# One layer of a diffusion backbone on one core: other weights in the list that orders the attention's instructions, and accumulators of two later stages on named banks in another turn

## The chip, the cores and the metric

One Trainium2 chip, one of its cores. The metric is the device time of one execution in microseconds (us); the median of several runs is compared. The engines are TensorE (PE: matmuls and transposes; PEld: its weight loads), VectorE (DVE), ScalarE (ACT), GpSimd (POOL) and SyncE (SP, which here only issues DMAs).

## What is computed

One layer over 1024 tokens of width 1024 with 256 context tokens, all in 32 bits:

```
h = x * (1 + scale1) + shift1                      # modulation from c
proj = h @ w_in + b_in                             # q, k, v of two branches, and gate logits
A: 8 heads, 2 kv heads, window of +-128 keys + 256 context keys, a sink logit per head
B: 8 heads, 2 kv heads, all 1024 keys + 256 context keys, RMS norm on q and k
y = (sig(ga) * (o_a @ w_branch_a) + sig(gb) * (o_b @ w_branch_b)) @ w_out
x = LN(alpha * x + gate1 * y)
h = x * (1 + scale2) + shift2
u = conv3(h @ w_up);  y = (silu(u_gate) * u_val) @ w_down
out = LN(alpha * x + gate2 * y)
```

## The kernel before, in words

A 32-bit product is made of three matmuls: each operand is split into a high part (a cast, `hi`) and a low part (operand minus high part, `lo`), and high*high, high*low and low*high are added in PSUM (`mm3`, L374 to L376). The splits are made by `split` (cast on L366, difference on L371) or, in attention, by lines of their own. PSUM has 8 banks; a tile of 128x512 fills one, a tile of 128x1024 two.

The stages run one after the other: projections and gates (0 to about 320 us of the span), attention (320 to 742), the rest of branch B's product and the output product with the first LayerNorm (742 to about 860), the up product with the convolution in 22 tiles (to about 1305), the down product and the last LayerNorm. PE runs through all of them with little idle time.

**Attention** is cut into 32 units: branch A's 16 (8 query blocks times 2 kv heads, four heads each), then branch B's 16. A unit's steps: POOL splits q (`qhi`, `qlo`, L723 and L726), PE turns it (`qtr`, L731), ACT copies it (L736), a DMA swaps its halves (`qdm`, L740); PE makes the scores of the four heads (`sc`, and in branch B `scx` for the context keys; L752 and L753); DVE scales them and takes the row minimum (`pm`, L786), ACT takes the exponential (`ex`, L795). Then, key block by key block (4 or 5 in branch A, 10 in branch B; "chunk" below), PE turns the probabilities (`tr`, L840, four transposes into one bank of the ring `pt`), the turned chunk is split, and PE multiplies it with the values (`av`, L849, one matmul for the high part and one for the low part, into the one bank `av0`). A chunk is split in one of two ways: ACT casts it out of PSUM (`hi`, L1218) and DVE subtracts (`lo`, L1224); or, for the chunks in the list `POOLED`, ACT copies it out of PSUM (`cp`, L1208) and POOL does both (`ph`, L1213, and `pl`, L1224). The first `av` of a unit starts the sum, so every other `av` of the unit is ordered behind the high part of chunk 0. At the end ACT copies the sum (`avs`, L1238), and POOL does a chain of five steps (`up` L1242, `ot` L854 twice, `tt` L1249, `oh` L866, `ol` L863). Between the units run 16 groups of branch A's output product, and at the end four of branch B's (`grp`, 12 matmuls each, tile `ptb`), whose gate is multiplied in by DVE (L1115).

The order of all this is made while the program is built. `graph` lists the operations, each with an engine, a cost and a key: the unit's number plus a weight from the list `KEY`. `plan` goes through them: for each engine it looks at the first `LOOK` operations in the order of their keys, takes those that could start within `SLACK` of the earliest, and of these the one with the least key. So a key is a priority among operations that could start at about the same time, not a date. `FILL` are the keys of the first and the last of branch A's groups. The resulting order on all five engines is fixed in the program; on the chip each engine goes through its list and waits where an operand is late.

**PSUM behind attention.** The pool `ps3` has two tags: `sml` (L1322; 2 slots of one bank) and `big` (L1319; 3 slots of two banks). In the program before, `sml` has the banks 0 and 1, and the three slots of `big` are the banks 2-3, 6-7 and 4-5, used in this turn. `big` is called 20 times: four accumulators of branch B's product, ten of the output product, and six of the first three tiles of the up product (gate and value of tiles 0, 1 and 2: `u0_0`, `u1_0`, `u0_1`, `u1_1`, `u0_2`, `u1_2`). The last three, `u1_1`, `u0_2` and `u1_2`, are on 4-5, 2-3 and 6-7. A `u` accumulator is read by one ACT instruction (L1688) and two DVE instructions (L1689, L1691) of `conv3`; then its banks are free.

From tile 3 on (`up_tile`, L1825 to L1857) a tile is seven products of four `mm3` each (A11, S2, S1, S3, A12, S4, A22: Strassen's scheme) in four accumulators a, b, c, d of one bank each. Their banks come from the list `PSU = 6, 7, 2, 3, 4, 5, 0, 1` (L50): tile 3 has a on 6, b on 7, c on 2, d on 3, and tile 4 has 4, 5, 0, 1. In this stage PE's order is that of the program; the other engines' order is arranged by the framework when the program is built.

Of the kernel before, what the change touches and what calls it, by code (L numbers as in the profile page):

```python
# [7 lines left out]
F32 = mybir.dt.float32  # L8
# [5 lines left out]
P = 128  # L14
D = 1024
T = 1024
# [23 lines left out]
PWB = 5  # L40
DAH = 3
SINK = 640
POOLED, FILL, SUMS = ((3,), (2, 6)), (16.13, 25.4), ('ot1', 'ot1')
LOOK, SLACK = 24, (0, 0, 0, 0.11, 0.209)
D3AT = (7, 5), (7, 9), (4, 1), (4, 4), (4, 7), (4, 10), (5, 2)
NXS = 5
RAWB = 3
# [38 lines left out]
def plan(ops, rings, free, look, slack):  # L86
    todo = [sorted((o for o in ops if o.eng == e), key=lambda o: o.key) for e in range(5)]
    for o in ops:
        for b in o.uses:
            b.left += 1  # L90
    port, done = 0.0, []
    while any(todo):
        best = None
        for e in range(5):
            ready = []
            for o in todo[e][:look]:
                if any(d.end is None for d in o.after):
                    continue
                r = max([free[e]] + [d.end for d in o.after] + [b.free(rings) for b in o.takes])
                if o.port:  # L100
                    r = max(r, port)
                if r < BIG:
                    ready.append((r, o))
            if ready:
                least = min(r for r, _ in ready) + slack[e]
                pick = min((c for c in ready if c[0] <= least), key=lambda c: c[1].key)
                if best is None or pick[0] < best[0]:
                    best = pick
        r, o = best
        todo[o.eng].remove(o)  # L110
        o.start, o.end = r, r + o.lat
        free[o.eng] = r + o.occ
        if o.port:
            port = r + o.occ
        for b in o.takes:
            b.slot = rings[b.ring].index(b.free(rings)) if b.fix is None else b.fix
            rings[b.ring][b.slot] = BIG
        for b in o.uses:
            b.left -= 1
            b.end = max(b.end, o.end)  # L120
            if b.left == 0:
                rings[b.ring][b.slot] = b.end
        done.append(o)
    return sorted(done, key=lambda o: o.start)
# [9 lines left out]
    tr=(PE, .436, .685), hi=(ACT, .47, .675), lo=(DVE, .605, .765), cp=(ACT, .47, .675), ph=(POOL, .59, .70),  # L134
# [9 lines left out]
PRING = "pt", "s", "av"  # L144
RINGS = dict(pt=3, s=2, av=1, qs=1, q1=2, q2=2, p=8, hi=4, lo=4, ptr=2, up=1, ot=1, rb=2, wraw=1, wh=1, wl=1)

KEY = {'qh': -2.206, 'qt': -0.961, 'sc': 0.037, 'scs': (0.029, 0.269),
           'scx': -0.548, 'tr': 0.763, 'tru': (0.17, 0.098),
           'av': 1.292, 'st': 1.191, 'out': 1.297, 'exd': 0.565, 'st1': 1.248, 'wb': (28.06, 28.638),
           'wg': (31.993, 33.356, 33.022, 33.265), 'ge': 1.33, 'gr': 4.033}  # L150
UNITS = 32


def graph(x, key=KEY, pooled=((3,), (2, 6)), fill=None, ot=("ot0", "ot1")):
    ops, last = [], {}
# [191 lines left out]
def rings():  # L347
    return {n: [0.0] * c for n, c in RINGS.items()}
# [3 lines left out]
def layer_kernel(  # L352
# [66 lines left out]
    def ht(name, shape=(P, T), dt=F32):  # L419
        hslot[name] = pool, tag = hfree.pop(0)  # L420
        return pool.tile(list(shape), dt, tag=tag, name=name, bufs=1)
# [38 lines left out]
    sc, scc = ht("sc"), ht("scc")  # L460
# [21 lines left out]
    st1 = {}  # L482
# [808 lines left out]
    rwb = {}  # L1291
    for o in plan(graph(Issue(), KEY, POOLED, FILL, SUMS)[0], rings(), [0.0, 2.2, 0.0, 0.0, 0.0], LOOK, SLACK):
        if o.fn:
# [18 lines left out]
    ps3 = tc.alloc_tile_pool(name="ps3", bufs=1, space=PSUM, reuse_waits="tile")  # L1312

    hfree += [(za, f"Z{n}") for n in range(16)]

    def tm(name, dt=F32, w=T):
        return post.tile([P, w], dt, tag="m", name=name, bufs=4)

    def big(name):  # L1319
        return ps3.tile([P, T], F32, tag="big", name=name, bufs=3)  # L1320

    def sml(name, w=512):  # L1322
        return ps3.tile([P, w], F32, tag="sml", name=name, bufs=2)
# [49 lines left out]
    wb = {2: [wq.tile([P, 8, P], R32, tag="w", name=f"{a}wb2", bufs=4) for a in "hl"]}  # L1373
# [3 lines left out]
    def both(f):  # L1377
        bT[1, f] = ht(f"bT1_{f}")
        nc.sync.dma_start(bT[1, f], sgd[KT + f])
        ps = big(f"b1_{f}")  # L1380
        w = wb[f // 2]
        for hf in (0, 1):
            for j in range(4):
                k = (f % 2) * 4 + j
                a = O[1, hf, 0, j // 2][:, j % 2], O[1, hf, 1, j // 2][:, j % 2]
                mm3(ps[:, hsl(hf)], (w[0][:, k], w[1][:, k]), a, j == 0, j == 3)
        nc.vector.tensor_tensor(out=bT[1, f], in0=ps, in1=bT[1, f], op=ALU.mult)
# [27 lines left out]
    def diag(cols, n, nm):  # L1415
        dg = tm(f"dg{nm}", w=HALF).rearrange("p (a b) -> p a b", b=P)
        i = nc.vector.tensor_tensor(out=dg[:, 0:n], in0=ident.unsqueeze(1).to_broadcast([P, n, P]),
                                    in1=cols.unsqueeze(2).to_broadcast([P, n, P]), op=ALU.mult)
        last_diag[:] = [i.ins]
        return dg[:, 0:n].rearrange("p a b -> p (a b)")  # L1420
# [7 lines left out]
    def ln_add(zf, zs, zq, s, first, nm, qe, se):  # L1428
        w = s.stop - s.start
        ln_flush()  # L1430
        if first:
            nc.scalar.activation(zq[:, s], zf, AF.Square)
            nc.gpsimd.tensor_scalar(out=zs[:, s], in0=zf, scalar1=1.0, scalar2=0.0, op0=ALU.mult, op1=ALU.add)
            return
        q = tm(f"sq{nm}", w=w)
        nc.scalar.activation(q, zf, AF.Square)
        se.tensor_tensor(out=zs[:, s], in0=zs[:, s], in1=zf, op=ALU.add)
        sqs.append(lambda: qe.tensor_tensor(out=zq[:, s], in0=zq[:, s], in1=q, op=ALU.add))
# [18 lines left out]
    def ln_steps(zs, zq, s, nm, emit, first, gap, gap1, gap2, each, pm=2, order=range(KT), behind=None):  # L1457
# [41 lines left out]
        def held(f):  # L1499
# [5 lines left out]
            for n, f in enumerate(order)]  # L1505

    zs, zq = tm("zs1"), tm("zq1")
    def wout_z(f, s, ps, first):
        nc.vector.scalar_tensor_tensor(out=zv(f, s), in0=ps, scalar=modc[:, 16 + f:17 + f], in1=zv(f, s),
# [99 lines left out]
    def y_pair(f, s, first=False):  # L1609
        w = s.stop - s.start  # L1610
        ps = big(f"y{f}_{s.start}_{w}")
        for ks in (range(6), range(6, KT)) if first and s.start == 0 else (range(KT),):
            for a in (0, 1):
                mm_ticked(ps[:, a * HALF:a * HALF + w], wts[f + a], mrg, s, ks)
        for a in (0, 1):
            wout_z(f + a, s, ps[:, a * HALF:a * HALF + w], first and a == 0)
# [94 lines left out]
    def up_start(j, gv):  # L1711
        if (j, gv) not in ups:
            if (j, gv) not in upw:
                up_weights(j, gv)
            ups[j, gv] = big(f"u{gv}_{j}"), upw.pop((j, gv)), set()
        return ups[j, gv]
# [45 lines left out]
    for k in range(4):  # L1762
        steps = build(k)
        n = 2 if k < 2 else 0
# [10 lines left out]
    ps3 = tc.alloc_tile_pool(name="ps3u", bufs=1, space=PSUM, reuse_waits="tile")  # L1775
# [415 lines left out]
```

## Time and profile before

| | us |
|---|---|
| median of 3 runs | 1541.86 (1540.32 to 1542.12) |
| profiled execution | 1540.56 |
| its span, from the first to the last instruction | 1538.8 |
| PE busy in the span | 1516.7 |
| DVE, ACT, POOL busy | 1142.5, 803.6, 780.6 |
| PE's longest wait, at about 941 us | 6.3 |

Views of the profile: *waits* lists who waited for whom; *windows* gives busy time of each engine in stretches of the span, with PE's granted clock (1.00 is full speed); *timeline* lists instructions in order of time (start, duration, engine, line, what it writes and reads, and in brackets the idle time before it and what ended it); *lines* groups instructions by line. An end of a matmul is modelled: the start of the next is the surer number.

### The profile page before, as it was taken

Reading aid. Unit: us, or ns where it says so; the run is one execution under the profiler, and the core shown is the slowest. Engines: PE = TensorE matmul, PEld = TensorE weight load, DVE = VectorE, ACT = ScalarE, POOL = GpSimd, SP = SyncE. Lnnn points to the kernel's source line nnn. Section 1 sums busy time; section 2 is a strip of 40 time slices with the busy share of each in tenths; the row PEclk is TensorE's granted clock in tenths of the full one; section 3 lists DMA queues with packets and bytes.
Section 4 is the critical chain, followed back from the end, with each engine's and each line's share of the span. In section 5 each row is a group of like instructions: output and inputs, shape, how many; then the busy total and the mean of one; then the engine's idle time right before and its main releaser. Section 6 shows DMA issues by size and latency. Waiting matters only on the chain.

```text
span 1538.8 us, 21952 instructions
## 1 busy us (share of the span) xinstructions
PE 1516.7 (99%) x7652; PEld 1271.8 (83%) x7652; DVE 1142.5 (74%) x1729; ACT 803.6 (52%) x1403; POOL 780.6 (51%) x741
## 2 busy tenths in 40 slices
PE   9999999999999999999999998999999999999997
PEld 7888888888988888888788986888888888888886
DVE  7588847628777777887656887788888787656797
ACT  5422223449977767898223563444444444435543
POOL 0375303428887565785334555666676675021063
PEclk9999999999999999999999999999999999999999
DMA  9667663312347573652471322233334446996733
GB/s 377 239 227 253 223 236 106 100 38 62 92 134 183 131 154 82 165 115 66 144 173 35 104 87 92 88 108 114 113 109 114 110 111 171 373 280 211 251 95 110
DMA packets 112161, 229.73 MB, mean 149 GB/s; under 512 B 13521, under 2 KB 27345, under 8 KB 111954
## 3 DMA queue, kind: packets, MB, share of 16 engines
q1 hardware_dynamic: 97040, 199.72, 39.7%
q0 software_dynamic: 10400, 20.19, 8.4%
q10 hardware_dynamic: 4610, 8.42, 1.5%
q8 instruction: 60, 0.98, 0.3%
q14 instruction: 51, 0.42, 0.1%
HBM read 177.09 MB, written 65.87 MB: 158 GB/s over the span
## 4 chain that ended last, share of the span: by engine, by line
PE 90%; DVE 4%; POOL 2%; issue 2%; ACT 1%; DMA 1%; DVEq 0%; SPq 0%; POOLq 0%; ACTq 0%
PE av L849 7%; PE pt L840 6%; PE g L376 4%; PE g L374 4%; PE g L375 4%; PE p L374 4%; PE p L376 4%; PE p L375 4%; PE s L752 3%; PE s L753 3%; PE a L374 2%; PE a L375 2%; PE a L376 2%; PE d L375 2%; PE c L375 2%; PE d L376 2%
## 5 line engine op out<-in xcount | busy, mean ns | idle before, releaser
L1224 DVE TENSOR_TENSOR lo<-pt,hi 128x512 fp32r<-128x512 f32 x188 | 126.1, 687 | 31.0 <-ACT hi L1218 28.5
L371 DVE TENSOR_TENSOR ld<-rd,hd 128x1024 fp32r<-128x1024 f32 x77 | 97.8, 1288 | 49.2 <-ACT hd L366 45.5
L1218 ACT CAST hi<-pt 128x512 fp32r<-128x512 f32 x188 | 108.4, 583 | 43.3 <-PE pt L840 38.1
L366 ACT CAST hd<-rd 128x1024 fp32r<-128x1024 f32 x77 | 79.6, 1052 | 84.7 <-PE p L376 60.4
L374 PE MATMUL p<-hd 128*128 128x512 f32 x264 | 103.3, 391 | 0.0
L375 PE MATMUL p<-ld,hd 128*128 128x512 f32 x264 | 102.8, 389 | 0.0
L376 PE MATMUL p<-hd,ld 128*128 128x512 f32 x264 | 102.7, 389 | 0.0
L849 PE MATMUL av<-lo,VT 128*128 128x512 f32 x236 | 100.8, 432 | 0.4 <-POOL lo L1224 0.4
L849 PE MATMUL av<-hi,VT 128*128 128x512 f32 x236 | 101.0, 435 | 0.2 <-ACT ptra L1238 0.2
L786 DVE TENSOR_SCALAR_CACHE_REDUCE p<-s,cvt,nmc 128x1024 f32<-128x1024 f32 x64 | 85.9, 1341 | 20.5 <-PE s L753 12.7
L376 PE MATMUL g<-hh,wlg 128*128 128x512 f32 x256 | 99.8, 390 | 0.4 <-POOL wlg L371 0.4
L374 PE MATMUL g<-hh,whg 128*128 128x512 f32 x256 | 100.0, 391 | 0.0
L375 PE MATMUL g<-hl,whg 128*128 128x512 f32 x256 | 99.6, 389 | 0.0
L371 POOL TENSOR_TENSOR wlg<-wg,whg 128x512 fp32r<-128x512 f32 x32 | 45.2, 1417 | 103.8 <-ACT whg L366 86.7
L795 ACT ACTIVATE p<-p,nm 128x1024 f32<-128x1024 f32 x64 | 74.1, 1158 | 17.7 <-DVE p L786 17.5
L840 PE MATMUL pt<-ident,p 128*128 128x128 f32 x512 | 76.6, 272 | 0.0
L840 PEld LDWEIGHTS pt<-ident,p 128*128 128x128 f32 x512 | 63.1, 140 | 15.7
L752 PE MATMUL s<-KL,q 128*128 128x512 f32 (+2 forms) x186 | 73.5, 395 | 0.0
L753 PE MATMUL s<-KL,q 128*128 128x512 f32 (+2 forms) x186 | 69.6, 374 | 0.5 <-DMA q<-q 0.5
L366 ACT CAST wS<-s 128x512 fp32r<-128x512 f32 x76 | 45.7, 623 | 44.7 <-POOL s L1523 41.9
L366 ACT CAST wA<-ru 128x512 fp32r<-128x512 f32 x57 | 35.6, 625 | 61.5 <-PE d L376 32.7
L786 DVE TENSOR_SCALAR_CACHE_REDUCE pa<-s,negsink 128x640 f32<-128x640 f32 (+1 forms) x58 | 49.2, 856 | 24.0 <-PE s L753 19.3
(436 smaller groups left out, 5030.7 us busy)
## 6 DMA issues: line engine op xcount, KB each, us to landing
wml<-in_wmodT_dram SPq DMA_DIRECT2D x48, 512.0 KB
ru<-in_w_up_dram SPq DMA_DIRECT2D x38, 512.0 KB
rd<-td SPq DMA_DIRECT2D x55, 256.0 KB
rd<-sd SPq DMA_DIRECT2D x44, 256.0 KB
rd<-in_w_dn_dram SPq DMA_DIRECT2D x33, 256.0 KB
wm<-in_wmodT_dram SPq DMA_DIRECT2D x16, 512.0 KB
wg<-in_w_g_dram SPq DMA_DIRECT2D x32, 256.0 KB
q<-q SPq DMA_DIRECT2D x64, 128.0 KB
```

Of the source, the lines that this page charges most:

```text
L366: cast[:] = [nc.scalar.copy(hi, src).ins]
L371: low[:] = [lo_eng.tensor_tensor(out=lo, in0=src, in1=hi.bitcast(F32), op=ALU.subtract).ins]
L374: nc.tensor.matmul(ps, a[0], b[0], start=start, stop=False, skip_group_check=resumed)
L375: nc.tensor.matmul(ps, a[0], b[1], start=False, stop=False, skip_group_check=resumed)
L376: return nc.tensor.matmul(ps, a[1], b[0], start=False, stop=stop, skip_group_check=resumed).ins
L752: nc.tensor.matmul(o, self.q1[:, hs], ks, start=True, stop=False)
L753: nc.tensor.matmul(o, self.q2[:, hs], ks, start=False, stop=stop)
L786: nc.vector.tensor_scalar(out=p if self.br else p[:, self.pad + 1:SINK + 1], in0=self.sv[h], scalar1=self.scale()[:, hs] if self.br else - ...
L840: nc.tensor.transpose(tr[:, h * P:(h + 1) * P], src, ident)
L849: nc.tensor.matmul(self.av, v, self.parts[n][low], start=first, stop=self.left == 0)
L1218: nc.scalar.copy(hi, units[u].parts[n])
L1224: e.tensor_tensor(out=lo, in0=src, in1=hi.bitcast(F32), op=ALU.subtract)
```

## The change

Two things. The weights of the planned order are replaced: `KEY`, `FILL`, `SLACK` and `POOLED`. And `big` gets three tags with one slot each in place of one tag with three; three empty tiles at the head of the pool `ps3` lay out their banks first, and a list says the turn: `big2`, `big0`, `big1`, and so on.

```diff
-POOLED, FILL, SUMS = ((3,), (2, 6)), (16.13, 25.4), ('ot1', 'ot1')
-LOOK, SLACK = 24, (0, 0, 0, 0.11, 0.209)
+POOLED, FILL, SUMS = ((0,), (1, 8)), (16.885703, 28.298765), ('ot1', 'ot1')
+LOOK, SLACK = 24, (0, 0, 0.031835, 0.0879, 0.031696)
...
-KEY = {'qh': -2.206, 'qt': -0.961, 'sc': 0.037, 'scs': (0.029, 0.269),
-           'scx': -0.548, 'tr': 0.763, 'tru': (0.17, 0.098),
-           'av': 1.292, 'st': 1.191, 'out': 1.297, 'exd': 0.565, 'st1': 1.248, 'wb': (28.06, 28.638),
-           'wg': (31.993, 33.356, 33.022, 33.265), 'ge': 1.33, 'gr': 4.033}
+KEY = {'qh': -1.21914, 'qt': -1.187093, 'sc': -0.106225, 'scs': (0.233244, 0.27861),
+           'scx': -1.945172, 'tr': 0.840531, 'tru': (0.122743, 0.070723),
+           'av': 1.36184, 'st': 1.192968, 'out': 0.661224, 'exd': 1.373419, 'st1': 1.769253, 'wb': (27.79832, 29.926055),
+           'wg': (31.897283, 33.009176, 33.189585, 33.435465), 'ge': 0.762978, 'gr': 4.580045}
...
+    bigs = [2, 0, 1]
+    for n in range(3):
+        ps3.tile([P, T], F32, tag=f"big{n}", name=f"bg{n}", bufs=1)
...
     def big(name):
-        return ps3.tile([P, T], F32, tag="big", name=name, bufs=3)
+        bigs.append(bigs.pop(0))
+        return ps3.tile([P, T], F32, tag=f"big{bigs[-1]}", name=name, bufs=1)
```

`POOLED` has one list for each branch (chunks of a unit, counted from 0). The pairs in `scs` and `tru` are branch A's and branch B's. `wb` and `wg` are the keys of the weight loads and of the groups of branch B's product at the end of attention.

## The prediction

> **What bounds the kernel now.** First the head of the page: PE is busy in 1516.7 us of 1538.8, so at most 22 us of idle time can go away, and work that PE has to do at its pace stays.
>
> ```profile
> span 1538.8 us, 21952 instructions
> PE 1516.7 (99%) x7652; PEld 1271.8 (83%) x7652; DVE 1142.5 (74%) x1729; ACT 803.6 (52%) x1403; POOL 780.6 (51%) x741
> ```
>
> Next the waits of PE, longest first (engine, line, whom it waited for, us, times, longest), which say where that idle time ends:
>
> ```profile
> PE a L374 <- DVE c L1691: 6.3, 1, 6.3
> PE b L374 <- POOL O L866: 1.2, 1, 1.2
> ...
> PE b L374 <- DVE bT L1115: 0.9, 1, 0.9
> PE s L753 <- DMA q<-q: 0.5, 1, 0.5
> PE av L849 <- POOL lo L1224: 0.4, 2, 0.3
> ```
>
> One wait stands out: the first up tile in Strassen's form (tile `a`) waits 6.3 us, once, for a convolution on DVE. Waits of attention (L753, L849) are below a microsecond each. Then busy time by stretch of attention and of what follows it (from:to, length, PE, PEld, DVE, ACT, POOL busy, granted clock, DMA share, GB/s):
>
> ```profile
> 320.00:360.00 40.00, 39.31 (x249) 34.83 (x249) 23.28 (x53) 27.08 (x61) 17.92 (x30) 1.00 0.15 37
> 360.00:400.00 40.00, 39.97 (x277) 36.19 (x276) 32.94 (x70) 35.92 (x81) 33.88 (x50) 1.00 0.32 81
> 400.00:440.00 40.00, 39.52 (x272) 35.40 (x271) 28.97 (x63) 35.10 (x79) 33.38 (x48) 1.00 0.38 105
> 440.00:480.00 40.00, 39.13 (x234) 32.16 (x233) 29.47 (x66) 30.83 (x71) 36.85 (x49) 1.00 0.65 167
> 480.00:640.00 160.00, 160.00 (x935) 134.50 (x934) 116.75 (x241) 115.09 (x247) 93.68 (x114) 1.00 0.53 129
> 640.00:720.00 80.00, 80.00 (x498) 67.03 (x497) 68.45 (x143) 72.13 (x163) 58.60 (x72) 1.00 0.52 120
> 720.00:742.00 22.00, 21.80 (x117) 17.96 (x116) 10.03 (x17) 11.19 (x23) 9.19 (x13) 1.00 0.11 34
> 742.00:755.00 13.00, 10.58 (x45) 7.86 (x44) 6.90 (x7) 2.21 (x3) 3.71 (x5) 1.00 0.62 230
> ```
>
> PE's idle time in attention is 0.69 + 0.03 + 0.48 + 0.87 = 2.1 us in branch A (to 480), 0.2 us in branch B (to 742), and 2.4 us where attention ends (742 to 755). No second engine is at its limit, but ACT and POOL come near it: 35.9 and 33.9 of 40 at 360 to 400, and at 440 to 480 POOL has 36.9 of 40.
>
> **The change, part by part. 1: the banks.** I follow the 20 calls of `big`. Before, the turn of the slots is 2-3, 6-7, 4-5; the twentieth accumulator, `u1_2`, has 6-7, and tile 3's `a` opens on bank 6. So PE can't begin tile 3 before DVE has read the very last convolution input. After, the empty tiles take 0-1, 2-3 and 4-5, so `sml` gets 6 and 7; call n (from 0) takes slot (n + 2) mod 3. `u1_1` (n = 17) gets 2-3, `u0_2` 4-5, `u1_2` 0-1. Tile 3's a and b (6, 7) then follow small LayerNorm tiles that are long done, c and d (2, 3) follow `u1_1`; `u1_2` is met first by tile 4's c, nine products (24.5 us, below) after PE's last `u` matmul instead of right behind it. Within `ps3` each call still takes the slot of the call three before it, so nothing else there waits for longer. The timeline of PE at this place:
>
> ```profile
> 940.64 0.39 PE L376 MATMUL u<-B,lwu 128*128 128x512 f32 x1
> 947.33 0.76 PE L374 MATMUL a<-B,wA 128*128 128x512 f32 x1 [6.30 <-DVE c L1691]
> ...
> 950.88 0.53 PE L376 MATMUL a<-B,wA 128*128 128x512 f32 x1
> 951.24 0.39 PE L374 MATMUL a<-B,wA 128*128 128x512 f32 x1
> 951.47 0.40 PE L375 MATMUL a<-B,wA 128*128 128x512 f32 x1
> ```
>
> The pitch from start to start is 0.23 us outside the wait (951.24 to 951.47; I reckon with 0.227, the mean over longer stretches). So PE was free at 940.64 + 0.227 = 940.87 and began at 947.33: **6.46 us**. And the nine matmuls from 947.33 to 951.24 took 3.91 us, where nine pitches are 2.04: **1.87 us** more. The granted clock says why:
>
> ```profile
> 941.00:947.30 6.30, 0.03 (x1) 0.00 (x1) 6.27 (x6) 2.35 (x4) 2.65 (x2) 0.76 0.32 87
> 947.30:951.30 4.00, 3.97 (x10) 3.18 (x11) 2.80 (x2) 0.00 (x0) 3.17 (x3) 0.52 0.69 263
> ```
>
> It is 0.76 on average in the wait and about half for 4 us behind it. The Trainium skill, "TensorE: Matmul & The Clock Gate", Part 1, says the gate halves the clock after an idle window of about 3.4 us and gives it back after about 3.4 us of work; by that the loss behind the wait would be an estimated 1.7 us, and the sum below 0.2 us smaller. The trace agrees within that; the measured 1.87 us stays.
>
> What is late next, if the bank no longer holds `a`? DVE's list there:
>
> ```profile
> 930.19 0.69 DVE L371 TENSOR_TENSOR wA<-ru,wA 128x512 fp32r<-128x512 f32 x1
> ...
> 939.56 2.97 DVE L371 TENSOR_TENSOR wS<-s,wS 128x512 fp32r<-128x512 f32 x3
> 942.45 1.75 DVE L371 TENSOR_TENSOR wA<-ru,wA 128x512 fp32r<-128x512 f32 x1
> ...
> 945.31 0.68 DVE L371 TENSOR_TENSOR wA<-ru,wA 128x512 fp32r<-128x512 f32 x1
> 945.91 1.27 DVE L1691 SCALAR_TENSOR_TENSOR c<-u,cvt,c 128x1023 f32<-128x1023 f32 x1
> ...
> 948.48 1.66 DVE L1702 TENSOR_TENSOR c<-c 128x512 f32<-128x512 f32 x1
> ```
>
> A11's weight is split by 930.9. A product is 12 matmuls, 2.72 us, so S2 would begin at 943.6, S1 at 946.3, S3 at 949.0, A12 at 951.8, A22 at 957.2. The three S splits end at 942.5 and the A splits at 946.0, all in time. `d` is full at 951.8 and must be read by DVE before A22: DVE's list ends at 950.1, with two additions of 0.69 us (as the first row, of the same shape) left, so by about 953, 4 us before it is needed. That list is the cover; were 4 us of DVE work put ahead of the read, A22 would begin to wait. Behind 951.5 no wait of PE over 0.2 us is in the list until the end, and loads of later weights start when PE frees their slots, so they move with it. I take the whole **-8.3 us**; 0 if the layout is not as I derive it.
>
> **2: the end of attention.** PE's timeline:
>
> ```profile
> 743.72 0.39 PE L376 MATMUL b<-O,lwb 128*128 128x512 f32 x1
> 745.26 0.49 PE L374 MATMUL b<-O,hwb 128*128 128x512 f32 x1 [1.15 <-POOL O L866]
> 746.07 0.50 PE L375 MATMUL b<-O,hwb 128*128 128x512 f32 x1 [0.32 <-POOL O L863]
> ...
> 752.59 0.39 PE L376 MATMUL b<-O,lwb 128*128 128x512 f32 x1
> 753.93 0.50 PE L374 MATMUL b<-O,hwb 128*128 128x512 f32 x1 [0.95 <-DVE bT L1115]
> ```
>
> By starts less the pitch these cost 1.31 + 0.58 + 1.11 = 3.0 us. The first two are POOL's chain behind the last `av`, the third a DVE list that starts behind the same chain. What covers the chain is groups that PE runs after the last `av`. Unit 31's last `av` had the key 31 + 1.292 + 9 x 0.098 = 33.17, and two groups of four had higher ones (33.27, 33.36); now it is 31 + 1.362 + 9 x 0.0707 = 33.00, and three have (33.01, 33.19, 33.44). Each is 12 x 0.227 = 2.7 us of cover. But a key only decides between operations that are ready, and an `av` that isn't gives way to a group. Bounds: -3.0 (all goes) and +2.7 (one group less of cover). I take **-1.0**, a third, since the third wait also hangs on a load behind the chain.
>
> **3: the rest of the order.** The counts stay: 32 units, one chunk of each unit of branch A on POOL and two of branch B, 20 groups. What moves is when PE waits. From below: all idle time of 320 to 742, 2.3 us. Besides, turns between transposes and products have a price:
>
> ```profile
> 729.03 0.48 PE L849 MATMUL av<-lo,VT 128*128 128x512 f32 x1
> 729.35 0.39 PE L849 MATMUL av<-hi,VT 128*128 128x512 f32 x1
> 729.58 0.60 PE L840 MATMUL pt<-ident,p 128*128 128x128 f32 x4
> ```
>
> The `av` behind four transposes holds PE for 0.32 us (729.03 to 729.35), the one behind it for 0.23: 0.09 us a turn. Were 30 of at most 236 such turns (two `av` to a chunk; 76 chunks in branch A, 160 in B) to go or come, it would be 2.7 us either way. From above, only rival E gives a price. q's split is asked for one unit later (-1.22 for -2.21) and its turn earlier: less time for POOL, ACT and the DMA, whose worst effect now is the 0.5 us row of L753. The groups run on to key 28.3 in place of 25.4, where, at 640 to 720, ACT has 72.1 of 80: a little relief. I take **-0.5**, near the rows, which show little to win.
>
> Sum: -6.46 - 1.87 - 1.0 - 0.5 = -9.83. The profiled execution took 1540.56 (the span and 1.76 around it), so it would take 1530.7; the median of the runs is 1.30 above it, which makes **1532.0 us**.
>
> **The rivals.** A, the forecast: 1529 to 1535, chance 0.58.
>
> B: the banks bring 8.3, but the new order costs 2 to 5 us by more waits in branch A: 1535.5 to 1538.5. For it speaks that branch A's engines are tight; against it, that only 2.1 us are lost there now. 0.17.
>
> C: all idle time of parts 2 and 3 goes too: 1541.86 - 8.33 - 3.0 - 2.3 = 1528.2, down to 1526 with fewer turns. 0.13.
>
> D: the change doesn't do what it says: the allocation differs, tile 3 still waits on the last convolution, and only parts 2 and 3 remain: 1541.86 - 1.5 = 1540.4. Against it: the empty tiles are the pool's first, as in the later pool `ps3u`, where they got the banks in turn. 0.05.
>
> E, slower: branch A's chunk on POOL is now chunk 0, and every `av` of the unit is ordered behind its high part. The pieces:
>
> ```profile
> L1208 ACT COPY ptr<-pt 128x512 f32<-128x512 f32 x17 | 9.9, 581 | 3.6 <-PE pt L840 3.3
> L1218 ACT CAST hi<-pt 128x512 fp32r<-128x512 f32 x65 | 37.4, 582 | 8.7 <-PE pt L840 7.8
> L1213 POOL TENSOR_SCALAR hi<-ptr 128x512 fp32r<-128x512 f32 x17 | 10.6, 622 | 2.9 <-ACT ptr L1208 2.9
> L854 POOL TENSOR_TENSOR ot<-ptra,up 64x256 f32<-64x256 f32 x32 | 23.4, 731 | 2.3
> ```
>
> Its high part takes ACT's copy (0.58) and POOL's cast (0.62) where another chunk's takes ACT's cast alone (0.58): 0.62 us later, 0.7 with the hand-over, and another 0.73 for each POOL step it queues behind. The Trainium skill, "TensorE: Matmul & The Clock Gate", Part 1, calls GpSimd's queue strictly first in, first out, by which the cast can't pass such a step; no row here tests that. Uncovered in all 16 units it is 11.2 us: 1541.86 - 8.33 + 11.2 = 1544.7; behind one step, 22.9 us: 1556. It decides from (8.33 + 3.1) / 16 = 0.71 us a unit. Against it: while a unit's `av` wait, PE has the next unit's scores and the last one's products. 0.07.
>
> **How the numbers follow.** 0.2%, about what a measurement of this kernel can tell from no change, is 3.1 us: faster is under 1538.8, slower over 1544.9. Faster: A 0.58, B 0.16, C 0.13, D 0.01 = 0.88. Same: B 0.01, D 0.04, E 0.01 = 0.06. Slower: 0.06 of E. The range 1527 to 1538 leaves out D, E, the far half of C's lower end and the end of B, some 0.18.
>
> **What would show it.** Right: no row of waits for `a` on L1691, starts of `u` and `a` 0.23 us apart, the clock at 1.00 from 930 to 960; PE's rows of L866 and L1115 smaller; PE's idle time at 320 to 480 about 2 us. Wrong: `a`, or A22, waiting at that place (1); rows of L866 as large as now (2); PE waiting in branch A for ACT or POOL over 5 us in total, `av` for L1213 above all (3, B or E).

## The result and the profile after

| | before | changed |
|---|---|---|
| median, us (lowest to highest) | 1541.25 (1540.32 to 1542.12, 4 runs) | 1533.03 (1532.53 to 1534.34, 4 runs) |
| ratio, 95% interval | 1 | 0.9948 (0.9931 to 0.9965) |
| span of the profiled execution, us | 1538.8 | 1531.7 |

The changed kernel is 8.2 us faster by the medians; 9.8 were forecast, and the range held the time. The two profiled executions that are shown below differ by 7.1 us. The lines of L1319 and beyond are five higher in the changed kernel (conv3's L1691 is now L1696, the addition of the two branches, L1367, now L1372); attention's are the same.

The head of its page, and the first rows of its list of PE's waits (engine, line, whom it waited for, us, times, longest):

```profile
span 1531.7 us, 21972 instructions
PE 1512.8 (99%) x7652; PEld 1272.2 (83%) x7652; DVE 1144.3 (75%) x1729; ACT 801.2 (52%) x1403; POOL 772.2 (50%) x741
```

```profile
PE b L374 <- DVE bT L1115: 4.4, 2, 2.6
PE av L849 <- POOL hi L1213: 1.9, 2, 1.7
PE cb L517 <- DVE mhalf L402: 1.1, 1, 1.1
PE av L849 <- POOL lo L1224: 0.7, 1, 0.7
```

The row of 6.3 us for `a` is gone. In its place two rows have grown: the gate product of branch B (L1115) from 0.9 to 4.4 us, and POOL's part of attention from 0.4 us to 2.6. Tile 3's first product in PE's timeline of the changed kernel:

```profile
940.63 0.39 PE L376 MATMUL u<-B,lwu 128*128 128x512 f32 x1
940.86 0.39 PE L374 MATMUL a<-B,wA 128*128 128x512 f32 x1
...
943.58 0.39 PE L374 MATMUL b<-T24h,wS 128*128 128x512 f32 x1
```

From the last `u` to the first `a` is 0.23 us, one pitch, and S2 begins at 943.58 where 943.6 was forecast. The windows of the changed kernel (from:to, length, busy time of PE, PEld, DVE, ACT, POOL, granted clock, DMA share, GB/s), for attention, for the stretch behind it and for this place:

```profile
320.00:360.00 40.00, 39.83 (x253) 35.55 (x252) 22.45 (x51) 26.92 (x62) 19.46 (x32) 1.00 0.17 41
...
480.00:640.00 160.00, 157.61 (x924) 131.83 (x923) 117.04 (x243) 119.23 (x256) 94.74 (x117) 1.00 0.58 137
...
742.00:755.00 13.00, 8.60 (x34) 6.37 (x33) 8.56 (x9) 3.06 (x3) 3.97 (x4) 0.95 0.84 309
...
947.30:951.30 4.00, 4.00 (x20) 3.30 (x19) 2.45 (x2) 0.00 (x0) 3.69 (x3) 1.00 0.72 271
```

At 947.3 to 951.3 PE does 20 matmuls at full clock where it did 10 at about half. At 742 to 755, however, it now stands idle for 4.4 us instead of 2.4.

**Where the time went.** Four marks cut the two spans into pieces: the first `b` (attention is over), the first `y` (the output product begins), the first `a`, and the end. PE's timeline of before, then of the changed kernel:

```profile
742.59 0.39 PE L374 MATMUL b<-O,hwb 128*128 128x512 f32 x1
...
778.54 0.39 PE L374 MATMUL y<-mh,hwo 128*128 128x512 f32 x1
```

```profile
739.63 0.39 PE L374 MATMUL b<-O,hwb 128*128 128x512 f32 x1
...
747.04 0.50 PE L374 MATMUL b<-O,hwb 128*128 128x512 f32 x1 [1.81 <-DVE bT L1115]
...
750.12 0.39 PE L375 MATMUL b<-O,hwb 128*128 128x512 f32 x1
753.10 0.50 PE L374 MATMUL b<-O,hwb 128*128 128x512 f32 x1 [2.59 <-DVE bT L1115]
...
757.08 0.40 PE L375 MATMUL b<-O,hwb 128*128 128x512 f32 x1
...
778.87 0.39 PE L374 MATMUL y<-mh,hwo 128*128 128x512 f32 x1
```

| piece | before | changed | difference |
|---|---|---|---|
| to the first `b` | 742.59 | 739.63 | -2.96 |
| first `b` to first `y` | 35.95 | 39.24 | +3.29 |
| first `y` to first `a` (947.33, 940.86) | 168.79 | 161.99 | -6.80 |
| first `a` to the end | 591.47 | 590.84 | -0.63 |
| span | 1538.8 | 1531.7 | -7.1 |

The banks' term lies in the third piece (-6.46 of wait) and the fourth (-1.87 of slow clock). Attention became 3.0 us shorter, and the stage behind it gave just that back. The last piece is 1.2 us longer than the banks' term leaves it; that is within what executions differ by there (590.2 to 592.1 us in the ten profiled ones, of all experiments, in which `a` does not wait). The gain of attention is clear of such differences: the first `b` starts at 742.6 to 743.4 in the four profiled executions with the old weights, and at 739.6 to 741.6 in the eight with all the new ones.

**Why the stage behind attention gives it back.** All engines meet at one place. Before, in order of time (start, duration, engine, line, output and inputs, and in brackets the idle time before and its end):

```profile
745.29 0.73 POOL L863 TENSOR_TENSOR O<-ot,O 128x256 fp32r<-128x256 f32 x1
746.04 0.33 SPq L1331 DMA_DIRECT2D rwb<-in_w_b_dram  x1
747.55 0.69 DVE L1115 TENSOR_TENSOR bT<-b,bT 128x512 f32<-128x512 f32 x1 [2.61 <-PE b L376]
750.91 1.23 DVE L371 TENSOR_TENSOR lwb<-rwb,hwb 128x1024 fp32r<-128x1024 f32 x1 [2.67 <-ACT hwb L366]
...
753.19 0.69 DVE L1115 TENSOR_TENSOR bT<-b,bT 128x512 f32<-128x512 f32 x1
```

And the changed kernel:

```profile
739.65 0.74 POOL L863 TENSOR_TENSOR O<-ot,O 128x256 fp32r<-128x256 f32 x1
740.42 0.34 SPq L1336 DMA_DIRECT2D rwb<-in_w_b_dram  x1
744.08 1.05 ACT L366 CAST hwb<-rwb 128x1024 fp32r<-128x1024 f32 x1 [8.10 <-DMA rwb<-in_w_b_dram]
745.16 1.23 DVE L371 TENSOR_TENSOR lwb<-rwb,hwb 128x1024 fp32r<-128x1024 f32 x1 [4.64 <-ACT hwb L366]
746.31 0.68 DVE L1115 TENSOR_TENSOR bT<-b,bT 128x512 f32<-128x512 f32 x1
...
749.49 1.41 DVE L371 TENSOR_TENSOR lwo<-rwo,hwo 128x1024 fp32r<-128x1024 f32 x1 [1.24 <-ACT hwo L366]
...
752.37 1.28 DVE L1115 TENSOR_TENSOR bT<-b,bT 128x512 f32<-128x512 f32 x2
```

In both, the last weight load of branch B (`rwb`) is issued within 0.03 us of POOL's last step in attention. In the built program the memory of that load's tile lies over tiles of POOL's chain for the last unit (`up`, `ot`), and SyncE's instruction waits for POOL. (The trace shows this wait and no addresses; the experiment with other slots, below, tests the reason.) The load, ACT's cast and DVE's low part follow one another, so the low part `lwb` ends at 746.4. Before, DVE's list had the first gate product ahead of `lwb` and the second behind it; now the first is behind `lwb`. A group of `b` is full at about 742.3 and waits for 4 us, and PE, which has only the two accumulators of `sml` here, waits for the gate product to free one. The second gate product stands behind `lwo`, the next weight loaded late, in the same way.

The load itself has not fallen behind: it is issued 5.6 us earlier than before (740.42 for 746.04), and PE comes 3.0 us earlier. New is the place of the gate products in DVE's list. That list is arranged by the framework when the program is built, and it goes with the weights: every run here with old weights has the first gate product ahead of `lwb`, and every arranged one with the new weights that makes `lwb` on DVE has it behind. So what PE gains in attention it waits off here. By starts less the pitch the two waits are 1.97 and 2.75 us (747.04 less 744.84, and 753.10 less 750.12, less 0.227 each), and the slow clock behind the second (last section) costs 1.71: 6.4 us, where the three waits of before cost 3.0. That is the 3.29 of the table but for 0.1.

### The profile page after: what moved, and what is told of

It is laid out like the page before. It is cut to its first block, busy times and chain, and to the rows that moved or that the text cites. A ratio compares the mean times of both kernels' runs of the same rounds, so it can differ in the third digit from the quotient of the medians.

```text
span 1531.7 us, 21972 instructions
## 1 busy us (share of the span) xinstructions
PE 1512.8 (99%) x7652; PEld 1272.2 (83%) x7652; DVE 1144.3 (75%) x1729; ACT 801.2 (52%) x1403; POOL 772.2 (50%) x741
## 4 chain that ended last, share of the span: by engine, by line
PE 92%; DVE 3%; DMA 1%; POOL 1%; issue 1%; ACT 1%; SPq 0%; DVEq 0%; POOLq 0%; ACTq 0%
PE av L849 7%; PE pt L840 6%; PE g L376 4%; PE g L374 4%; PE g L375 4%; PE p L375 3%; PE p L374 3%; PE p L376 3%; PE s L752 3%; PE s L753 3%; PE c L376 2%; PE d L376 2%; PE a L376 2%; PE d L375 2%; PE a L375 2%; PE c L375 2%
## 5 line engine op out<-in xcount | busy, mean ns | idle before, releaser
L371 DVE TENSOR_TENSOR wS<-s,wS 128x512 fp32r<-128x512 f32 x57 | 53.5, 966 | 16.6 <-ACT wS L366 16.6
```

The source lines that it names most:

```text
L371: low[:] = [lo_eng.tensor_tensor(out=lo, in0=src, in1=hi.bitcast(F32), op=ALU.subtract).ins]
```

## The experiments

Each edit is to the changed kernel unless it says otherwise, and every ratio is to before's own median in the same series (1540.85, 1541.03 or 1541.30; 1541.25 beside the changed kernel). Differences to the changed kernel are across series, and so good to about half a microsecond more than the intervals say.

**The two parts apart.** First the old weights with the new banks: `KEY`, `FILL`, `SLACK` and `POOLED` as in before.

```diff
-POOLED, FILL, SUMS = ((0,), (1, 8)), (16.885703, 28.298765), ('ot1', 'ot1')
-LOOK, SLACK = 24, (0, 0, 0.031835, 0.0879, 0.031696)
+POOLED, FILL, SUMS = ((3,), (2, 6)), (16.13, 25.4), ('ot1', 'ot1')
+LOOK, SLACK = 24, (0, 0, 0, 0.11, 0.209)
...
```

> The kernel before with the named banks alone, its old order of attention. My theory: the 6.46 us wait of the first up tile and the 1.87 us at half clock behind it go, nothing else moves: about 8.3 us under the kernel before, 1533.0 us, and PE still waits 3.0 us where attention ends. Rival (the weights carry the gain): less than 3 us under the kernel before, over 1538.

Measured: 1532.60 us (1532.08 to 1533.96), ratio 0.9944 (0.9931 to 0.9958). The banks alone bring 8.25 us, all that the whole change brings. In its list of PE's waits no row for `a` is left, and the row at the end of attention is smaller than in the changed kernel:

```profile
PE b L374 <- DVE bT L1115: 1.7, 2, 0.9
```

Then the new weights with the old `big`:

```diff
-        bigs.append(bigs.pop(0))
-        return ps3.tile([P, T], F32, tag=f"big{bigs[-1]}", name=name, bufs=1)
+        return ps3.tile([P, T], F32, tag="big", name=name, bufs=3)
```

> The new weights with the old banks. My theory: attention ends about 3 us earlier, the waits of L1115 behind it (4.4 us and half clock) give all of that back, and the first up tile waits about 6.4 us again: within 1 us of the kernel before, about 1541. Rival (the weights carry half of the gain or more): 1537 or less.

Measured: 1541.91 us (1539.37 to 1545.83), ratio 1.0007 (0.9998 to 1.0016): no difference. Its list of waits has both, 5.9 us for `a` and 4.5 us for L1115. The new order by itself, with this kernel behind it, is worth nothing.

**Is it the bank that held `a`?** Tile 3's `a` is put on bank 0, which belongs to `u1_2`, the last convolution's accumulator, in the changed kernel (tile 4's `c` takes bank 6 in exchange):

```diff
-PSU = 6, 7, 2, 3, 4, 5, 0, 1
+PSU = 0, 7, 2, 3, 4, 5, 6, 1
```

> The changed kernel with one entry of the bank list turned, so that the third up tile's a lies on bank 0, which the last u accumulator has there, and the fourth's d on bank 6. My theory (what counts is which accumulator held a's bank): PE waits about 6.4 us for L1691 again, with the slow clock behind it, 8.3 us over the changed kernel, 1541.3. Rival (the tags, or the order that the other engines got with them, removed the wait): within 1 us of the changed kernel, 1533.

Measured: 1541.24 us (1539.46 to 1548.53), ratio 1.0006 (0.9995 to 1.0017), 8.2 us above the changed kernel. PE's timeline there:

```profile
945.78 0.77 PE L374 MATMUL a<-B,wA 128*128 128x512 f32 x1 [5.91 <-DVE c L1696]
```

From the first `y` to the end, where wait and slow clock lie, its profiled execution is 7.7 us longer than the changed kernel's. The one bank carries the difference, with nothing else of the change undone.

**The stage behind attention.** Four experiments ask what makes PE wait for L1115. First, the low part of the last `wb` goes to POOL, so that it can't stand ahead of a gate product on DVE:

```diff
-            wb[3] = weight(w_b[3], "wb3", 8, he=nc.scalar, le=nc.vector, rtag=None)
+            wb[3] = weight(w_b[3], "wb3", 8, he=nc.scalar, le=nc.gpsimd, rtag=None)
```

> The changed kernel with the low part of the last block of branch B's weights (lwb of block 3) made by POOL in place of DVE. My theory: this difference, held up by its late load, stands in DVE's list ahead of the gate products (L1115) that free the small accumulators; off that list, the waits of 1.97 and 2.5 us and the slow clock behind them (1.7 us) go: 5 to 6.4 us under the changed kernel, 1527 to 1528. Rival (the gate products are late for another reason, as their own loads): within 1 us of the changed kernel, 1533.

Measured: 1534.42 us (1532.62 to 1537.35), ratio 0.9956 (0.9944 to 0.9969), as the changed kernel: a miss. DVE's timeline shows why:

```profile
743.32 0.69 DVE L1115 TENSOR_TENSOR bT<-b,bT 128x512 f32<-128x512 f32 x1 [2.03 <-PE b L376]
750.19 1.23 DVE L371 TENSOR_TENSOR lwo<-rwo,hwo 128x1024 fp32r<-128x1024 f32 x1 [4.91 <-ACT hwo L366]
...
752.88 1.28 DVE L1115 TENSOR_TENSOR bT<-b,bT 128x512 f32<-128x512 f32 x2
```

The first gate product is now in time (743.32), and the next ones stand behind `lwo`, the next low part of a late load. PE's waits then have

```profile
PE b L374 <- DVE bT L1115: 4.4, 1, 4.4
```

one wait in place of two of 1.8 and 2.6 us, with the same sum. The culprit is not one instruction but each low part of a late load.

Next, the last two groups of `b` get accumulators of their own out of `big`, so that PE needs no gate product to go on:

```diff
-    bigs = [2, 0, 1]
+    bigs = [0, 1, 2]
...
-            rest(f, sml)
+            rest(f, sml if f < 2 else lambda nm: big(nm)[:, 0:HALF])
```

> The changed kernel with four accumulators in place of two for the rest of branch B's product: the third and the fourth go to two large slots that are idle there, and the turn of the slots is shifted so that all later tiles keep their banks. My theory: PE no longer has to wait for the gate products of the first two (L1115), which stand behind late weight splits in DVE's list: about 4.5 us of waits and the 1.7 us at half clock go, 6.2 us under the changed kernel, 1526.9. Rival (the same DVE list holds up what comes next, the merged tiles that the output product reads): within 2 us of the changed kernel, 1531 to 1533.

Measured: 1530.56 us (1528.60 to 1531.80), ratio 0.9934 (0.9921 to 0.9946), 2.5 us below the changed kernel, where 6.2 were forecast: between theory and rival. The row of L1115 is gone, but two small ones have come:

```profile
PE y L375 <- DVE ml L371: 0.6, 1, 0.6
...
PE y L376 <- DVE lwo L371: 0.3, 1, 0.3
```

Its first `a` starts at 937.62, 3.2 us earlier than the changed kernel's 940.86. The marks tell where the rest is. From first `b` to first `y` it takes 32.64 us, 6.60 less than the changed kernel: the gate products held PE, and all that was to be had there came. But from first `y` to first `a` it takes 1.56 us more, 0.9 of them in the two rows above: the output product meets late operands (`ml`, `lwo`) itself. And the first `b` comes 1.80 us later, at 741.43: in this execution 3.4 us at half clock followed a wait in attention (last section), in a part of the program that the edit doesn't touch.

Then DVE is held to the order of the program in this stretch, which has the four gate products of L1115 ahead of the low part of the last `wb` and of the late `wo`:

```diff
+    inturn = ExitStack()
+    inturn.enter_context(tc.manual_schedule(engines={mybir.EngineType.DVE}))
     for f in range(KT):
...
+    inturn.close()
```

> The changed kernel with DVE's list of that stage (rest of branch B's product and merging) in the order of the program in place of the arranged one, so that each gate product (L1115) stands ahead of the weight splits that come with later loads. My theory (the place in DVE's list is the cause, not the two accumulators as such): PE's waits for L1115 shrink to under 1 us, 5 to 6 us under the changed kernel, 1527 to 1528. Rival (too few accumulators whatever the order, since each merge has DVE wait for a cast of ACT): PE still waits 3 us or more there, 1531 or more.

Measured: 1544.52 us (1542.73 to 1548.82), ratio 1.0025 (1.0016 to 1.0035), 11.5 us above the changed kernel. PE's waits:

```profile
PE y L376 <- DVE lwo L371: 9.1, 1, 9.1
PE b L374 <- DVE bT L1115: 5.3, 1, 5.3
```

The theory fell here, and the rival held: the program's order is no cure. The first gate product is in time now, but the second stands behind a low part of another kind, `ml`, whose operand is cast by ACT; and in ACT's list that cast stands behind `hwo`, the cast of a late load. ACT's timeline, then DVE's:

```profile
750.44 1.04 ACT L366 CAST hwo<-rwo 128x1024 fp32r<-128x1024 f32 x1 [4.29 <-DMA rwo<-in_w_out_dram]
751.39 1.04 ACT L366 CAST mh<-bT 128x1024 fp32r<-128x1024 f32 x1
```

```profile
752.46 1.23 DVE L371 TENSOR_TENSOR ml<-bT,mh 128x1024 fp32r<-128x1024 f32 x1 [7.07 <-ACT mh L366]
753.61 0.68 DVE L1115 TENSOR_TENSOR bT<-b,bT 128x512 f32<-128x512 f32 x1
```

In both lists that were tried, a late load holds up the next gate product or operand. The list of before was not tried with the new weights. By the changed kernel's own rows, with a sum (L1372) and the second gate product right behind `lwb`, the latter would end at about 748.2, where PE would be there at 747.8: an estimate of 0.4 us of wait in place of 4.7. So it is not shown that the order of DVE's list has no part in this. The next experiment leaves that list and moves the loads.

So last, the loads themselves. Empty tiles fix the addresses of the pool's slots, and the late weights take the slots whose memory attention gives up first:

```diff
+    for n in range(16):
+        za.tile([P, T], F32, tag=f"Z{n}", name=f"zb{n}", bufs=1)
...
+            first = [f"Z{n}" for n in (14, 15, 9, 10, 8, 13, 12, 11, 7, 6, 5, 4, 3, 2)]
+            hfree.sort(key=lambda h: first.index(h[1]) if h[1] in first else 99)
             wb[3] = weight(w_b[3], "wb3", 8, he=nc.scalar, le=nc.vector, rtag=None)
```

> The changed kernel with the slots for the loads behind attention taken in another turn: the block of branch B's weights and the first block of the output weights land on memory that attention gave up earlier, in place of memory under the last unit's tiles (up, ot, rb), which POOL reads until its chain ends. Two accumulators, as in the changed kernel. My theory: these loads set out only when POOL's last step is done (740.4 in the changed kernel), and so the splits that stand ahead of the gate products in DVE's list are late; with early loads PE's waits for L1115 (4.4 us) and the slow clock go, 5 to 6 us under the changed kernel, 1527 to 1528. Rival (DVE's list is too long in itself): the waits stay over 3 us, 1531 or more.

Measured: **1527.02 us** (1525.66 to 1527.67), ratio 0.9908 (0.9894 to 0.9921). It beats both kernels: 14.3 us below before, 6.0 below the changed kernel. In its timeline of the same place the load (L1338 here) starts 13.4 us earlier, and DVE, in the same order as in the changed kernel, is not held by a load:

```profile
727.01 0.58 SPq L1338 DMA_DIRECT2D rwb<-in_w_b_dram  x1
740.76 1.22 DVE L371 TENSOR_TENSOR lwb<-rwb,hwb 128x1024 fp32r<-128x1024 f32 x1
742.88 0.69 DVE L1115 TENSOR_TENSOR bT<-b,bT 128x512 f32<-128x512 f32 x1 [0.90 <-PE b L376]
```

Its windows show PE busy through the whole stretch, at full clock:

```profile
742.00:755.00 13.00, 13.00 (x59) 10.78 (x58) 12.00 (x12) 3.91 (x4) 2.21 (x4) 1.00 0.33 106
```

Its first `y` starts at 772.59, 6.28 us before the changed kernel's 778.87, though attention ended no earlier (first `b` at 739.95). So with this list the late loads are the cause, and the list is not too long in itself. The four accumulators on top of it:

> Early slots and four accumulators together, on the changed kernel. My theory: what four accumulators left (0.9 us of waits of the output product for DVE, and the slow stretch behind) goes as well: 1 to 2 us under four accumulators alone (1530.6), 1528 to 1529, and no better than early slots alone by more than 1 us. Rival (the two fixes hit different waits): 1526 or less.

Measured: 1527.74 us (1526.09 to 1529.07), ratio 0.9912 (0.9898 to 0.9925): the same as with the slots alone. Both edits take away the same wait, and nothing is left for the second.

**What the new order is worth when nothing takes it back.** The old weights with the new banks and four accumulators, then with the early slots as well:

> The named banks and four accumulators with the old weights. It tells what the new order of attention is worth once the stage behind it lets the gain through. My theory: the new order ends attention 3 us earlier, so this is 3 us slower than the changed kernel with four accumulators, about 1530, and 2 us under the banks alone (1532.6), whose waits for L1115 were 1.7 us. Rival (the new order is worth nothing by itself): equal to the changed kernel with four accumulators within 1 us.

Measured: 1532.22 us (1530.83 to 1532.62), ratio 0.9942 (0.9930 to 0.9955), 1.7 us above the new weights with the same accumulators (1530.56); the two intervals overlap, so this run alone doesn't settle it. The 2 us under the banks alone that were forecast did not come.

> Named banks, four accumulators and early slots with the old weights. My theory: attention's end sets the time of what follows in both orders now, and the new order's attention is 3 us shorter, so this is 2 to 3 us slower than the same with the new weights. Rival (the new order is worth nothing once its stage behind is mended): equal within 1 us.

Measured: 1532.15 us (1530.80 to 1532.41), ratio 0.9940 (0.9927 to 0.9952), 4.4 us above the new weights with the same two edits (1527.74, 0.9912, 0.9898 to 0.9925). The intervals don't touch: with the loads early, the new order is worth about 4 us, more than the 2 to 3 that were forecast. Of this, attention is 2.8 (first `b` at 739.91 for 742.72), and 1.1 lie between first `b` and first `y` (32.64 us for 33.74), where the old order still waits 0.8 us for a gate product and 0.3 for POOL. With the old weights neither the four accumulators nor both edits together changed the median by as much as half a microsecond from the banks alone (1532.60).

**The chunk on POOL.** Chunk 3 in place of chunk 0 for branch A, as in the old weights:

```diff
-POOLED, FILL, SUMS = ((0,), (1, 8)), (16.885703, 28.298765), ('ot1', 'ot1')
+POOLED, FILL, SUMS = ((3,), (1, 8)), (16.885703, 28.298765), ('ot1', 'ot1')
```

> The changed kernel with branch A's chunk 3 on POOL, as before, in place of chunk 0; all other new weights stay. By the forecast, chunk 0 on POOL costs nothing that PE sees: within 2 us of the changed kernel, 1531 to 1535. By rival E, every product of a unit is late by 0.7 us with chunk 0 on POOL: 5 us or more faster than the changed kernel, 1528 or less.

Measured: 1538.83 us (1536.59 to 1542.99), ratio 0.9990 (0.9980 to 1.0000), 5.8 us *above* the changed kernel. Its waits:

```profile
PE b L374 <- DVE bT L1115: 4.1, 3, 2.5
PE av L849 <- POOL hi L1213: 4.0, 2, 2.4
PE av L849 <- POOL lo L1224: 2.7, 2, 2.1
```

Both the forecast and rival E missed: not only did chunk 0 on POOL cost nothing, with these weights its place is better than chunk 3's. The loss lies in attention: the first `b` starts at 747.98, 8.35 us later than in the changed kernel. The two rows for POOL are 4.1 us larger, the first `b` itself waits 0.8, and behind the waits of 2.05 and 2.39 us for POOL PE ran at half clock for 3.4 us each time (from 475.3 and from 605.0), which costs 1.7 us apiece.

## Why the prediction came out right, point by point

**The banks** (-8.3): right in mechanism and size. The wait went to one pitch, the clock at 947 to 951 was 1.00, S2 started when forecast, and neither `a` nor A22 met anything late. Alone they measured -8.25, and putting `a` back behind the last convolution gave +8.2. Rival D, that the layout might not be as derived, is refuted by the same two runs.

**The end of attention** (-1.0): this step failed. "A third" of 3.0 us of waits was to go; instead the stretch from first `b` to first `y` grew by 3.29. The two waits for POOL's chain did go, as the extra cover was to make them: 24 matmuls of `ptb` run behind the last `av` where 12 did, one group more (the keys alone would have given three groups for two). The step named the third wait's cause, "a load behind the chain", and then let it count only as a reason to take a third; that DVE's list behind attention would be arranged otherwise under the new weights it did not consider. That was the whole matter: the wait for L1115 grew from 1.11 us to 1.97 and 2.75 (starts less the pitch), because the gate products now stand behind the low parts `lwb` and `lwo`, and their loads still start only at POOL's last step. With the same list and early loads the waits are gone. The upper bound, +2.7 for one group less of cover, was of the wrong mechanism and 0.6 short.

**The rest of the order** (-0.5): the direction was right and the size wrong. Attention ended 2.96 us earlier. It did not come from idle time as the windows count it: branch A's fell from 2.1 us to 0.2 (39.83 of 40 in its first window, the others full), but branch B's rose from 0.2 to 2.4 at 480 to 640, where PE waits for POOL's high part. The number of turns between transposes and products is no explanation either: products follow transposes 176 times before and 175 after. So the gain lies mostly in how closely PE's instructions follow each other. Counted from each one's start to the next one's, the steps behind the 32 small transposes of the row sums (L817) fell from 2.62 us to 0.97, two waits of 0.5 us in all among them, and those behind the turns of q (L731) from 9.80 to 8.91; the rest is spread. Which weight makes it was not separated.

**The sum**: -1.0 and -0.5 were forecast for steps 2 and 3, and the pieces show +3.3 and -3.0. Two errors of opposite sign nearly cancel, which is why the total of 9.8 came out 1.6 too large and no worse. That much is luck. Rival B named the right outcome for the order, a gain eaten by new waits, in the wrong place (branch A). Rival C, all idle time gone, was 1528.2: with the loads early the kernel takes 1527.0, so its time was there to be had. The 3.0 us at the end of attention went as it counted; the 2.3 in attention did not, as PE still waits 2.6 us for POOL there, and closer steps made up for them. Rival E, slower by chunk 0 on POOL, has the opposite sign in the run that tests it.

## What to carry to other kernels

When an earlier stage gets another order, look at how the lists of the other engines behind it come out: here products that PE needs fell behind work on a load whose memory still belonged to the last step of the stage before. Where a transfer is issued the instant some engine's last step ends, ask whether memory binds it to that step: here, to place its target over something freed earlier took away the whole wait, 6.0 us of the kernel's time, with DVE's list as it was. And ask which bank a stage opens on: the accumulator that the stage before reads last should be the one that the next stage meets last.

## What the hardware showed that was not expected

Two waits of 1.81 and 2.59 us, with 3.5 us of work between them (747.04 to about 750.5), were followed by the half clock. The window behind the second one in the changed kernel, and the one that holds the first:

```profile
745.00:750.30 5.30, 3.49 (x16) 2.55 (x14) 3.86 (x4) 2.03 (x3) 1.09 (x2) 1.00 1.01 399
...
753.10:757.00 3.90, 3.90 (x10) 3.09 (x11) 3.90 (x4) 1.84 (x2) 0.62 (x1) 0.56 0.68 181
```

The clock stayed at 1.00 through the first wait and fell to 0.56 behind the second: from 753.10 to 757.08 ten pitches took 3.98 us in place of 2.27, a loss of 1.7 us, which is part of the 3.29. The half clock set in at about 753.6, half a microsecond after PE was back at work, and held to 757.0. Before, waits of 1.15 and 0.95 us at this place left it alone. The Trainium skill, "TensorE: Matmul & The Clock Gate", Part 1, puts the drop behind an idle window of about 3.4 us; this trace does not agree, as no single wait here was that long. Nor does the length of the wait decide alone. In attention PE waits for POOL twice within 1.6 us at one place, and does so alike in the changed kernel and in the run with four accumulators (for each of the two, the first wait and a window behind both):

```profile
597.35 0.50 PE L849 MATMUL av<-hi,VT 128*128 128x512 f32 x1 [1.73 <-POOL hi L1213]
599.20:602.50 3.30, 3.30 (x23) 2.78 (x23) 2.01 (x4) 1.99 (x5) 0.38 (x1) 1.00 0.73 220
```

```profile
596.87 0.50 PE L849 MATMUL av<-hi,VT 128*128 128x512 f32 x1 [1.69 <-POOL hi L1213]
599.20:602.50 3.30, 3.30 (x13) 2.70 (x12) 0.86 (x3) 1.18 (x2) 0.00 (x0) 0.50 0.72 236
```

The second wait is 0.66 us in both. One execution goes on at full clock, the other at half. Of the eight profiled executions with all the new weights, three have this half clock (behind waits of 1.58, 1.69 and 2.14 us) and five do not (1.55 to 1.94). What decides, no run here tells. For the kernel it means that a wait of 1.6 to 2.1 us at this place can cost another 1.7 us, in one execution and not in the next.
